# Rotary embedding on one core: loads on SyncE's queue and stores on ScalarE's, in place of both on SyncE's in a fixed order

## The chip, the cores and the metric

The kernel runs on one core of a Trainium2 chip. The metric is the device time of one execution in microseconds. "Before" and "after" are the kernels without and with the change. A core has five engines that run their own programs and meet at semaphores: TensorE (PE), VectorE (DVE), ScalarE (ACT), GpSimd (POOL) and SyncE (SP). Transfers between HBM and the on-chip memory SBUF are issued by an engine's program into that engine's queue, and carried out by 16 DMA engines.

## The reference

The input is 16 batches of 512 positions of 1024 values, which are 16 heads of 64. Each head's first half x1 and second half x2 are rotated by an angle that depends on the position alone; the output has the shape (16, 512, 16, 64), float32.

```python
x = x.reshape(batch, seq, num_heads, head_dim)
x1, x2 = (x[..., :half_dim].copy(), x[..., half_dim:].copy())
cos = cos[None, :, None, :].copy()
sin = sin[None, :, None, :].copy()
rotated = np.concatenate([x1 * cos - x2 * sin, x1 * sin + x2 * cos], axis=-1)
```

## The kernel before

One tile c is one batch: 128 partitions of 4 positions of 1024 values (16 KB per partition, 2 MB in all). A unit u is one of the tile's four rows, 128 x 1024 values; there are NU = 64 units in NC = 16 tiles. The ring x_sb holds 40 units, that is ten tiles; the result is written over the input in the ring and stored from there.

For every unit, t1 = x * cos goes to PSUM (L232, VectorE, "mul") and t2 = swapped x * signed sin goes to t2_sb (L201, GpSimd; for u % 8 = 3, VectorE in L223). Then they are added. For u % 8 in (1, 3, 6) TensorE adds t2 to t1 in PSUM by a matmul with the identity (L172), and ScalarE copies the sum to the ring (L152). For the other units VectorE adds (L243, "comb"). VectorE's program is one list: mul(u), then comb(u - 2), so that the additions of a tile's last two units stand behind the first multiplications of the next tile. A t1 buffer comes free after the addition or the copy of the unit three before it; a t2 buffer after the one six before it.

All transfers are issued by SyncE (on_sync, L120 to L141) into one queue, in an order that is written out: load 0, the two tables, loads 1 to 9, then stores 0, 1 and 2, and from there load c + 8 behind store c for c = 2 to 7, then the stores 8 to 15. A store waits for all additions of its tile (wait_added, L104 to L109: sem_a counts ScalarE's copies, sem_v VectorE's additions). Load c waits from c = 10 on for store c - 10 to land, since it takes that tile's place in the ring. The stores 0 to 5 have semaphores of their own (sem_out), the last ten share sem_rest, for which SyncE waits at its end (L141).

Of the kernel before, what the change touches and what calls it, by code (L numbers as in the profile page):

```python
# [6 lines left out]
def bass_split_heads_rope_kernel(  # L7
# [19 lines left out]
    R = 4  # L27
# [8 lines left out]
    RING = 40  # L36
    NC = batch
    NU = batch * R

    def where(u):  # L40
        return u // R, u % R, u % RING
# [19 lines left out]
    with ExitStack() as stack:  # L61
        x_sb = stack.enter_context(nc.sbuf_tensor([P, RING, H, 2, HALF], fp32))
        t2_sb = stack.enter_context(nc.sbuf_tensor([P, NT2, H, 2, HALF], fp32))
        stage = stack.enter_context(nc.sbuf_tensor([P, 2, R * HALF], fp32))
# [6 lines left out]
        sem_out = [stack.enter_context(nc.semaphore(f"out{c}")) for c in range(NC - RING // R)]  # L71
        sem_rest = stack.enter_context(nc.semaphore("rest"))
        sem_cos = stack.enter_context(nc.semaphore("cos"))
        sem_sin = stack.enter_context(nc.semaphore("sin"))
# [16 lines left out]
        ov = out.rearrange("b (p r) h d -> b p (r h d)", r=R)  # L91
        xs = x_sb[:].rearrange("p n h t d -> p n (h t d)")

        def tile(c):
            k = c * R % RING
            return x_sb[:, k:k + R].rearrange("p n h t d -> p (n h t d)")
# [7 lines left out]
        def wait_added(eng, u):  # L104

            if n_pe[u]:
                eng.wait_ge(sem_a, n_pe[u])
            if n_comb[u]:
                eng.wait_ge(sem_v, n_comb[u])  # L109
# [8 lines left out]
                    eng.wait_ge(sem_v, n_comb[v])  # L118

        def on_sync(sp):  # L120
            AHEAD = 3

            def load(c):
                if c * R >= RING:
                    sp.wait_ge(sem_out[c - RING // R], 16)
                sp.dma_start(tile(c), xv[c]).then_inc(sem_in[c], 16)  # L126

            def store(c):
                wait_added(sp, c * R + R - 1)
                sp.dma_start(ov[c], tile(c)).then_inc(sem_out[c] if c < len(sem_out) else sem_rest, 16)  # L130

            load(0)
            for i, (table, sem) in enumerate(((cos, sem_cos), (sin, sem_sin))):
                sp.dma_start(stage[:, i, :], table.rearrange("(p r) d -> p (r d)", r=R)).then_inc(sem, 16)  # L134
            for c in range(1, RING // R):
                load(c)
            for c in range(NC):
                store(c)
                if AHEAD <= c + 1 < AHEAD + len(sem_out):
                    load(c + 1 - AHEAD + RING // R)  # L140
            sp.wait_ge(sem_rest, 16 * (NC - len(sem_out)))  # L141

        def on_scalar(ae):
            ae.wait_ge(sem_sin, 16)
            sv = stage[:, 1, :].rearrange("s (r d) -> s r d", d=HALF)
            ae.activation(s_sb[:, :, 0, :], sv, COPY, scale=-1.0)  # L146
            ae.activation(s_sb[:, :, 1, :], sv, COPY).then_inc(sem_s, 1)  # L147
            for u in range(NU):
                k = where(u)[2]
                if PE2[u]:  # L150
                    ae.wait_ge(sem_e, n_pe[u])
                    ae.activation(xs[:, k, :], t1_ps[:, u % NT1, :], COPY).then_inc(sem_a, 1)  # L152

        def on_tensor(pe):
            pe.wait_ge(sem_z, 1)
            for k in range(NT1):
                for b in range(EH):
                    pe.matmul(  # L158
                        t1_ps[:, k, b * BANK:(b + 1) * BANK], zero[:, 0:P], zero[:], start=True, stop=True
                    ).then_inc(sem_w, 1)  # L160
            pe.wait_ge(sem_i, 2)
            for u in range(NU):
                if not PE2[u]:
                    continue
                pe.wait_ge(sem_m, u + 1)
                if V2[u]:
                    pe.wait_ge(sem_d, n_dve[u])
                else:
                    pe.wait_ge(sem_p, n_pool[u])
                t2 = t2_sb[:, u % NT2, :, :, :].rearrange("p h t d -> p (h t d)")  # L170
                for b in range(EH):
                    ins = pe.matmul(  # L172
                        t1_ps[:, u % NT1, b * BANK:(b + 1) * BANK],
                        ident[:],
                        t2[:, b * BANK:(b + 1) * BANK],
                        start=False,
                        stop=True,
                        skip_group_check=True,
                    )
                ins.then_inc(sem_e, 1)  # L180
# [24 lines left out]
        def on_vector(ve):  # L205
# [44 lines left out]
            for u in range(NU + LEAD):  # L250
                if u < NU:
                    mul(u)
                if u >= LEAD and not PE2[u - LEAD]:
                    comb(u - LEAD)

        on_sync(nc.sync)
        on_scalar(nc.scalar)
        on_gpsimd(nc.gpsimd)
        on_tensor(nc.tensor)
# [34 lines left out]
```

## Time and profile before

| what | value |
|---|---|
| time, median of 3 runs | 163.88 us (163.47 to 164.49) |
| time of the profiled execution | 163.88 us |
| its span, first to last instruction | 162.5 us |
| DVE busy | 131.9 us (81%) |
| POOL busy | 130.6 us (80%) |
| PE busy | 84.9 us (52%) |
| ACT busy | 26.3 us (16%) |
| bytes moved | 67.26 MB, mean 414 GB/s |
| SyncE's queue, share of the 16 DMA engines' time | 97.7% |
| TensorE's granted clock, mean | 0.657 of full speed |

The span is what the profile covers; the time has a little more around it (163.88 less 162.5 is 1.4 us). A busy time is the union of an engine's own instructions, without its waits. Issuing a transfer isn't counted as busy. "Time to landing" of a transfer runs from its issue until its semaphore is full, and so holds the time that it stood in the queue.

### The profile page before, as it was taken

The page shows a single profiled execution, that of the slowest core. Times are in us where ns is not written, and L with a number is a line of the kernel's source. Part 1 is how long each engine was busy: PE and PEld are TensorE (multiplying, and loading weights), DVE is VectorE, ACT ScalarE, POOL GpSimd, SP SyncE. Part 2 cuts the span into 40 slices and gives each one's busy share as a digit, 9 for nine tenths or more (in the row PEclk, how much of TensorE's full clock was granted, in tenths as well). Part 3 has the DMA queues.
Part 4 walks back from the last instruction along what each step waited for, and adds up shares of the span by engine and source line. Part 5 has one row for each costly group of instructions (what it writes and reads, how often), then busy time and mean ns, then how long its engine had stood idle before and what let it go on. Part 6 is the DMA issues. An engine that isn't in the chain of part 4 may idle for free.

```text
span 162.5 us, 607 instructions
## 1 busy us (share of the span) xinstructions
PE 84.9 (52%) x102; PEld 26.7 (16%) x102; DVE 131.9 (81%) x116; ACT 26.3 (16%) x27; POOL 130.6 (80%) x62
## 2 busy tenths in 40 slices
PE   6003919346746745854745854664864584584000
PEld 1002402211211220220221220121121022021000
DVE  0079299998999979996999789996999899998600
ACT  3010220222022022022202112202102202201200
POOL 1059999999999999999989999799879997970000
PEclk9999995585557655557655558555559555869855
DMA  4999999999999999999999999999999999999993
GB/s 145 403 453 432 420 440 432 415 444 428 411 452 395 436 452 413 424 436 415 430 436 420 420 440 411 424 448 407 432 436 428 424 440 432 415 444 440 411 440 141
DMA packets 4898, 67.26 MB, mean 414 GB/s; under 512 B 544, under 2 KB 800, under 8 KB 800
## 3 DMA queue, kind: packets, MB, share of 16 engines
q1 hardware_dynamic: 4896, 67.24, 97.7%
q14 instruction: 2, 0.02, 0.0%
HBM read 33.69 MB, written 33.55 MB: 414 GB/s over the span
## 4 chain that ended last, share of the span: by engine, by line
DVE 27%; PE 22%; issue 19%; POOL 14%; ACT 6%; DMA 5%; SPq 0%; DVEq 0%; POOLq 0%
PE t_ps L172 22%; DVE x_sb L243 14%; POOL t_sb L201 14%; DVE t_ps L232 9%; ACT x_sb L152 6%; DMA stage<-in_sin_dram 5%; DVE t_sb L223 4%; SPq L134 0%; SPq L126 0%; ACT s_sb L146 0%; ACT s_sb L147 0%; DVEq L242 0%; DVEq L231 0%; DVEq L229 0%; POOLq L116 0%
## 5 line engine op out<-in xcount | busy, mean ns | idle before, releaser
L201 POOL TENSOR_TENSOR t_sb<-x_sb,s_sb 128x1024 f32<-128x1024 f32 x56 | 129.9, 2355 | 13.8 <-ACT s_sb L147 8.6
L172 PE MATMUL t_ps<-t_sb,ident 128*128 128x512 f32 x96 | 82.1, 1009 | 64.1 <-DVE t_ps L232 50.7
L232 DVE TENSOR_TENSOR t_ps<-x_sb,tab_ps 128x1024 f32<-128x1024 f32 x64 | 77.5, 1227 | 12.1 <-ACT x_sb L152 10.1
L243 DVE TENSOR_TENSOR x_sb<-t_ps,t_sb 128x1024 f32<-128x1024 f32 x40 | 48.6, 1217 | 0.0
L172 PEld LDWEIGHTS t_ps<-t_sb,ident 128*128 128x128 f32 x96 | 25.9, 296 | 120.4 <-DVE t_ps L232 85.7
L152 ACT ACTIVATE x_sb<-t_ps 128x1024 f32<-128x1024 f32 x24 | 24.6, 1023 | 116.9 <-PE t_ps L172 116.9
L223 DVE TENSOR_TENSOR t_sb<-x_sb,tab_ps 128x1024 f32<-128x1024 f32 x8 | 9.7, 1210 | 0.0
L210 DVE COPY tab_ps<-stage 128x128 f32<-128x128 f32 x1 | 0.3, 294 | 7.9 <-DMA stage<-in_cos_dram 7.9
L158 PE MATMUL t_ps<-zero 128*128 128x512 bf16 x6 | 2.7, 630 | 1.3 <-DVE zero L206 1.3
L146 ACT ACTIVATE s_sb<-stage 128x128 f32<-128x128 f32 x1 | 0.3, 309 | 7.3 <-DMA stage<-in_sin_dram 7.3
L146 ACT ACT_TABLE_LOAD x1 | 1.3, 1283 | 0.8 <-PEq L276 0.8
L158 PEld LDWEIGHTS t_ps<-zero 128*128 128x128 bf16 x6 | 0.7, 138 | 2.4 <-DVE zero L206 1.2
L206 DVE MEMSET zero<- 128x256 uint32 x1 | 0.3, 272 | 0.9 <-PEq L276 0.9
L183 POOL MEMSET ident<- 128x128 f32 x1 | 0.2, 204 | 0.3 <-POOLq L276 0.3
L185 POOL TENSOR_SCALAR_AFFINE_SELECT ident<-ident 128x128 f32<-128x128 f32 x1 | 0.3, 292 | 0.1
L276 POOL MEMSET const-float32-0.0<- 128x1 f32 x1 | 0.1, 98 | 0.3 <-issue 0.3
L212 DVE TENSOR_SCALAR tab_ps<-stage 128x128 f32<-128x128 f32 x1 | 0.3, 295 | 0.0
L147 ACT ACTIVATE s_sb<-stage 128x128 f32<-128x128 f32 x1 | 0.3, 293 | 0.0
L213 DVE COPY tab_ps<-stage 128x128 f32<-128x128 f32 x1 | 0.3, 283 | 0.0
L276 POOL MEMSET const-bfloat16-1.0<- 128x1 bf16 x1 | 0.1, 101 | 0.0
L276 POOL MEMSET const-uint8-127<- 128x1 uint8 x1 | 0.1, 101 | 0.0
L276 POOL MEMSET const-float32-1.0<- 128x1 f32 x1 | 0.1, 98 | 0.0
## 6 DMA issues: line engine op xcount, KB each, us to landing
x_sb<-in_x_dram SPq DMA_DIRECT2D x16, 2048.0 KB, 25.2
out_dram<-x_sb SPq DMA_DIRECT2D x16, 2048.0 KB, 26.9
stage<-in_cos_dram SPq DMA_DIRECT2D x1, 64.0 KB, 7.9
stage<-in_sin_dram SPq DMA_DIRECT2D x1, 64.0 KB, 7.6
```

The costliest lines, as they stand in the source:

```text
L146: ae.activation(s_sb[:, :, 0, :], sv, COPY, scale=-1.0)
L147: ae.activation(s_sb[:, :, 1, :], sv, COPY).then_inc(sem_s, 1)
L152: ae.activation(xs[:, k, :], t1_ps[:, u % NT1, :], COPY).then_inc(sem_a, 1)
L158: pe.matmul(t1_ps[:, k, b * BANK:(b + 1) * BANK], zero[:, 0:P], zero[:], start=True, stop=True).then_inc(sem_w, 1)
L172: ins = pe.matmul(t1_ps[:, u % NT1, b * BANK:(b + 1) * BANK], ident[:], t2[:, b * BANK:(b + 1) * BANK], start=False, stop=True, skip_group ...
L185: pl.affine_select(out=ident[:], in_=ident[:], compare_op=mybir.AluOpType.is_equal, fill=0.0, base=0, pattern=[[-1, P]], channel_multiplier=1,
L201: pl.tensor_tensor(t2_sb[:, u % NT2, :, :, :], swapped(k), sin_of(s_sb, r), mult).then_inc(sem_p, 1)
L206: ve.memset(zero[:], 0.0).then_inc(sem_z, 1)
L223: ve.tensor_tensor(t2_sb[:, u % NT2, :, :, :], swapped(k), sin_of(s_ps, r), mult).then_inc(sem_d, 1)
L232: ve.tensor_tensor(t1_ps[:, u % NT1, :].rearrange("p (h d) -> p h d", d=HALF), x_sb[:, k, :, :, :].rearrange("p h t d -> p (h t) d"), c_ps ...
L243: ve.tensor_tensor(xs[:, k, :], t1_ps[:, u % NT1, :], t2_sb[:, u % NT2, :, :, :].rearrange("p h t d -> p (h t d)"), add,).then_inc(sem_v, 1)
L276: nc = _bacc.Bacc("TRN2", target_bir_lowering=False, num_devices=1)
```

## The change

SyncE's program now holds the loads alone, in the order of the tiles, with the two tables behind load 0 as before; load c still waits for store c - 10 from c = 10 on. The stores are issued by ScalarE into its own queue: after the last unit of a tile ScalarE waits for all additions of that tile and issues the store. The wait for the last ten stores stays at the end of SyncE's program. No arithmetic is changed: the instructions of TensorE, VectorE and GpSimd are the same and stand in the same order.

```diff
         def on_sync(sp):
-            AHEAD = 3
-
-            def load(c):
+            for c in range(NC):
                 if c * R >= RING:
                     sp.wait_ge(sem_out[c - RING // R], 16)
                 sp.dma_start(tile(c), xv[c]).then_inc(sem_in[c], 16)
-
-            def store(c):
-                wait_added(sp, c * R + R - 1)
-                sp.dma_start(ov[c], tile(c)).then_inc(sem_out[c] if c < len(sem_out) else sem_rest, 16)
-
-            load(0)
-            for i, (table, sem) in enumerate(((cos, sem_cos), (sin, sem_sin))):
-                sp.dma_start(stage[:, i, :], table.rearrange("(p r) d -> p (r d)", r=R)).then_inc(sem, 16)
-            for c in range(1, RING // R):
-                load(c)
-            for c in range(NC):
-                store(c)
-                if AHEAD <= c + 1 < AHEAD + len(sem_out):
-                    load(c + 1 - AHEAD + RING // R)
+                if c == 0:
+                    for i, (table, sem) in enumerate(((cos, sem_cos), (sin, sem_sin))):
+                        sp.dma_start(
+                            stage[:, i, :], table.rearrange("(p r) d -> p (r d)", r=R)
+                        ).then_inc(sem, 16)
             sp.wait_ge(sem_rest, 16 * (NC - len(sem_out)))
 
         def on_scalar(ae):
...
             for u in range(NU):
-                k = where(u)[2]
+                c, r, k = where(u)
                 if PE2[u]:
                     ae.wait_ge(sem_e, n_pe[u])
                     ae.activation(xs[:, k, :], t1_ps[:, u % NT1, :], COPY).then_inc(sem_a, 1)
+                if r == R - 1:
+                    wait_added(ae, u)
+                    ae.dma_start(ov[c], tile(c)).then_inc(sem_out[c] if c < len(sem_out) else sem_rest, 16)
```

## The prediction, made before the changed kernel was run

> **What bounds the kernel now.** I read the page's DMA part first, because a kernel that moves 67 MB and does three elementwise operations per value is likely to stand there.
>
> ```profile
> span 162.5 us, 607 instructions
> ...
> DMA  4999999999999999999999999999999999999993
> ...
> DMA packets 4898, 67.26 MB, mean 414 GB/s; under 512 B 544, under 2 KB 800, under 8 KB 800
> ...
> q1 hardware_dynamic: 4896, 67.24, 97.7%
> ```
>
> All 38 inner slices have the 16 DMA engines at 90% or more, and one queue, SyncE's, carries it all for 97.7% of the span. The kernel is bound by bytes. But what else ends late? The waits of SyncE's queue and two instruction groups tell it.
>
> ```profile
> SPq L109 <- DVE x_sb L243: 73.7, 10, 13.4
> SPq L126 <- DMA out_dram<-x_sb: 52.7, 6, 17.4
> SPq L141 <- DMA out_dram<-x_sb: 9.2, 1, 9.2
> ```
>
> ```profile
> L201 POOL TENSOR_TENSOR t_sb<-x_sb,s_sb 128x1024 f32<-128x1024 f32 x56 | 129.9, 2355 | 13.8 <-ACT s_sb L147 8.6
> ...
> L232 DVE TENSOR_TENSOR t_ps<-x_sb,tab_ps 128x1024 f32<-128x1024 f32 x64 | 77.5, 1227 | 12.1 <-ACT x_sb L152 10.1
> L243 DVE TENSOR_TENSOR x_sb<-t_ps,t_sb 128x1024 f32<-128x1024 f32 x40 | 48.6, 1217 | 0.0
> ```
>
> The reader is to see that the last wait (L141) is 9.2 us, no more than a queued store or two: when the last store is issued, the arithmetic is done and the bytes aren't. POOL is busy 129.9 us and idle 13.8, of which 8.6 come before the tables are there, so arithmetic runs without a pause too. The timeline of SyncE's queue gives its pace: store 0 is issued at 22.2 us, store 13 at 137.92, so (137.92 - 22.2)/13 = 8.9 us per tile, and the last store at 152.92. So two chains end close together: arithmetic at 152.9 and one more store, the bytes at 162.4. A change that helps the bytes soon meets the arithmetic; one that delays the loads soon delays both.
>
> The pace of the bytes comes from issue times and the time to landing, asked for single transfers. Their last lines, for load 1, load 9, store 2, load 15 and store 15, with the issue at 2.18, 6.53, 40.48, 98.49 and 152.92:
>
> ```profile
> DMA to landing us min/median/max: 12.0/12.0/12.0
> DMA to landing us min/median/max: 46.8/46.8/46.8
> DMA to landing us min/median/max: 27.7/27.7/27.7
> DMA to landing us min/median/max: 25.1/25.1/25.1
> DMA to landing us min/median/max: 9.5/9.5/9.5
> ```
>
> They land at 14.2, 53.3, 68.2, 123.6 and 162.4. Eight loads in a row take (53.3 - 14.2)/8 = 4.89 us each. The last eight stores take (162.4 - 123.6)/8 = 4.85. Between them, where load and store take turns, eleven transfers take (123.6 - 68.2)/11 = 5.04, some 0.15 more each. This view of the end shows where that goes:
>
> ```profile
> core 0: us, PE busy (x) PEld busy (x) DVE busy (x) ACT busy (x) POOL busy (x), PEclk, DMA share, GB/s
> ...
> 124.00:152.00 28.00, 15.52 (x20) 4.82 (x20) 26.04 (x24) 5.13 (x6) 19.95 (x9) 0.70 1.00 430
> ...
> 158.00:162.50 4.50, 0.00 (x0) 0.00 (x0) 0.00 (x0) 0.00 (x0) 0.00 (x0) 0.50 0.40 171
> ```
>
> At the end only 0.40 of the engines' time is used: most DMA engines finish near 160, a few near 162.4. These few fell behind in the stretch of turns.
>
> **The change part by part.** *Stores leave SyncE for ScalarE's queue.* Sixteen issues of 0.34 us (median of L130) move. ScalarE is busy 26.3 us, so 16 x 0.34 = 5.4 us fit. What stands behind them is the copy of L152, for which VectorE already waits 10.1 us. Of the three TensorE units in eight, only the one with u % 8 = 1 comes right behind an odd tile's store. That store waits for the addition which VectorE makes directly after the multiplication that starts TensorE: 1.22 us plus 0.34 is 1.6, against up to 3.8 us of matmuls for one unit in the timeline. So the cost is 0, covered by TensorE; were the cover gone, 8 odd tiles x 0.34 = 2.7 us of VectorE. From below, nothing can be gained here. I take 0.
>
> *The wait of the tail.* It stood at the end of SyncE's program (L141) and still stands there; nothing is queued behind it. Cost 0.
>
> *Loads leave the hand-written order.* Load c now waits only for store c - 10, and nothing of SyncE's waits for arithmetic. Before, loads 1 to 9 ran alone until 53.3 us while store 0, issued at 22.2, waited 36.0 us to land. Afterwards store 0 begins near 24. No trace here shows two queues at work together; I bound the sharing by loads first and stores first, and take halves, since loads and stores have packets of one size (67.1 MB in the 4096 that aren't small, 16 KB each). Then load 3 still lands at 24 and load 4 at about 31; after that a load lands every 2 x 4.89 = 9.8 us, load 15 at 31 + 11 x 9.8 = 139 instead of 123.6.
>
> Is that in time? A store hangs on the next load: VectorE's program puts a tile's last additions (L243) behind the first multiplications (L232) of the next tile, so for an odd tile two of each, 4.9 us, and for an even tile 2.4 us, follow the next load. Load 14 (129) allows store 13 at 134, against 137.92 from the pace; load 15 (139) allows store 14 at 142, against 146.96; tile 15 itself needs four of POOL's 2.36 us and an addition, 10.9 us, so 150 against 152.92. Each has 3 to 5 us in hand. Load 10 waits for store 0, which lands near 36, some 45 us before load 10's turn. So nothing starves at halves, and the sum stays with the bytes.
>
> *Turns become a mixture.* From 24 us to load 15, loads 4 to 15 run beside as many stores: 24 transfers instead of 11 in which both directions meet. The nearest row is the stretch of turns, 0.15 us a transfer. Lower bound 0: both directions cost nothing together, and the 11 x 0.15 = 1.7 us of today vanish. Upper bound: the worst step in that stretch, load 13 after store 5 or so, about 5.4 us against 4.89, is 0.5 each, 12 us. I take 0.15, because it is a mean over eleven: 24 x 0.15 = 3.6, less today's 1.7, makes +1.9 us. With it load 15 lands near 142.5, and tile 15 would be stored at 153.4 where the pace says 152.9: the two meet, and starving adds at most 0.5, which the queue's own backlog covers.
>
> The sum: 162.5 + 1.9 = 164.4 us of span. The profiled execution took 163.88, so 1.4 us lie around the span; it is also the median of the runs (163.47 to 164.49). Forecast 165.8 us.
>
> A rule speaks against the 0.15. The Trainium skill, page "DMA: Bandwidth & Descriptors", section "Latency and other measured facts", has copies of this very tile size through sync and scalar queues at 214 GB/s in each direction at once, when the rows don't alias. That would be 428 GB/s in sum, the rate that the windows above show for stores alone (430), and hence no price for the mixture; the sum by the rule would be 162.1. The same page, section "Queues, rings and completion order", lets each DMA engine take its queues in turn, packet by packet, which would make my halves right; no trace here shows it yet.
>
> **The rivals.**
>
> *Stores crowd out loads (slower still).* If the second queue gets more than half, stores take all that arithmetic hands them: 4.9 of every 8.9 us, and a load lands every 8.9/4.0 x 4.9 = 10.9 us. Load c + 1 then overtakes the pace: it lands at 33 + 10.9 (c - 3), and 4.9 us later must not exceed 22.2 + 8.9c, which fails from c = 9. From there every tile costs two transfers, 9.8 us: store 14 at 102.3 + 5 x 9.8 = 151, tile 15 at 160, its store lands 7 later, 167; with the mixture's 1.9, 169, in time 170.4. For it: POOL has hardly any idle time to catch up with. Against it: equal packets, and a starving arithmetic hands out fewer stores, which gives the loads room.
>
> *The mixture is free, or better than turns (faster).* The place is the end, the 4.5 us with 0.40 of the DMA engines. If each DMA engine always has work of both kinds, none need fall behind, and today's 1.7 us go: 160.7 of span, 162.1 in time. It can't get much lower: arithmetic ends at 152.9 and one store alone takes 4.9 us plus issue and completion (load 0, the only transfer into an idle queue, took 8.1 in all), some 160. The case decides when the mixture costs under 0.02 us a transfer (24 x 0.02 = 0.5 against 1.7, that is 161.3). For it: at 124 to 152 the engines run at 1.00 without any loss, while a few still lag 3 us. Against it: only unmixed stretches are without loss.
>
> *Nothing changes.* The same bytes at the same share, between 0.02 and 0.13 us a transfer: span 161.3 to 163.9, times 162.7 to 165.3. For it: 97.7% of DMA time is used either way.
>
> *ScalarE as the new bottleneck.* If an issue blocks as load 9's did (2.08 us, with nine transfers ahead of it), 8 x (1.22 + 2.08 - 3.8), which is below 0, still hides; only with faster matmuls (2 us) does it cost 8 x 1.3 = 10 us. The store queue never holds more than two or three, so I give it little: some 171.
>
> **How the numbers follow.** A measurement of this kernel can tell about 1% from no change, 1.6 us. Forecast (mixture at 0.13 to 0.3 us a transfer, 165.3 to 169.4): 0.42. Stores crowding out loads: 0.10. ScalarE: 0.03. Mixture free: 0.15. Nothing changes: 0.30. Within 1% means 162.2 to 165.5, so 0.02 of the forecast and 0.01 of the free mixture count to the middle: faster 0.14, same 0.33, slower 0.53. The likeliest one's own range is 165.3 to 169.4; the whole one goes from 161.8 (between the free mixture's 162.1 and its floor, 160 and 1.4) to 170.5 (stores first).
>
> **What would show it.** Right: two queues with about half the packets each, load 15 landing at 139 to 143, loads that land before arithmetic asks for them, the last store issued at 152 to 154, transfers in the mixed stretch costing 5.0 us each, and some DMA engines more than 3 us behind at the end. Wrong: POOL idle for loads in the second half (stores first), VectorE's wait for ScalarE well over 10.1 us, an end near 160.5 with an even finish of the DMA engines, or a pace of packets in the mixture that isn't that of either stretch before.

## The result, and the profile after

The changed kernel takes 161.97 us (161.75 to 162.11, 4 runs) against 163.69 (163.47 to 164.49, 4 runs) for the kernel before: a ratio of 0.9885, 95% interval 0.9848 to 0.9922. It is 1.2% faster, where 1.2% slower was forecast. The profiled executions took 161.94 and 163.88 us, with spans of 160.5 and 162.5: 2.0 us less.

The page of the kernel after, the lines that answer to those of before:

```profile
span 160.5 us, 607 instructions
...
DMA  5999999999999999999999999999999999999996
...
DMA packets 4899, 67.27 MB, mean 419 GB/s; under 512 B 544, under 2 KB 800, under 8 KB 800
...
q1 hardware_dynamic: 2592, 33.69, 49.9%
q10 hardware_dynamic: 2304, 33.56, 48.8%
...
L193 POOL TENSOR_TENSOR t_sb<-x_sb,s_sb 128x1024 f32<-128x1024 f32 x56 | 129.6, 2376 | 17.0 <-DMA x_sb<-in_x_dram 8.9
L224 DVE TENSOR_TENSOR t_ps<-x_sb,tab_ps 128x1024 f32<-128x1024 f32 x64 | 77.1, 1227 | 10.4 <-ACT x_sb L141 8.6
```

Two queues now carry half of the bytes each, with the DMA engines at 90% or more in every inner slice, as before. POOL waits 8.9 us for loads, for which it never waited before; VectorE waits 8.6 us for ScalarE, no more than the 10.1 of before.

The pace in the mixture, from loads 4 and 15 (issued at 3.87 and 86.17 us), and the end, from store 15 (issued at 150.47). The last line of each answer has the time from issue to landing:

```profile
DMA to landing us min/median/max: 27.3/27.3/27.3
DMA to landing us min/median/max: 52.5/52.5/52.5
DMA to landing us min/median/max: 10.0/10.0/10.0
```

Load 4 lands at 31.2, load 15 at 138.7, store 15 at 160.5. Eleven loads and as many stores share (138.7 - 31.2) = 107.5 us, 4.89 per transfer. That is the pace of loads alone before (4.89) and not that of the turns (5.04). The busy time by stage shows where the two kernels differ. First before, the stretch of turns and two windows at the end of the span:

```profile
core 0: us, PE busy (x) PEld busy (x) DVE busy (x) ACT busy (x) POOL busy (x), PEclk, DMA share, GB/s
...
68.00:124.00 56.00, 33.33 (x38) 9.86 (x36) 51.14 (x45) 10.22 (x10) 51.87 (x23) 0.57 1.01 427
...
160.00:161.00 1.00, 0.00 (x0) 0.00 (x0) 0.00 (x0) 0.00 (x0) 0.00 (x0) 0.50 0.31 131
161.00:162.50 1.50, 0.00 (x0) 0.00 (x0) 0.00 (x0) 0.00 (x0) 0.00 (x0) 0.50 0.05 22
```

and after, the mixture and the end:

```profile
core 0: us, PE busy (x) PEld busy (x) DVE busy (x) ACT busy (x) POOL busy (x), PEclk, DMA share, GB/s
...
40.00:124.00 84.00, 49.11 (x59) 15.38 (x60) 79.33 (x69) 14.32 (x14) 78.33 (x35) 0.63 1.01 431
158.00:160.50 2.50, 0.00 (x0) 0.00 (x0) 0.00 (x0) 0.00 (x0) 0.00 (x0) 0.50 0.51 216
...
160.00:161.00 1.00, 0.00 (x0) 0.00 (x0) 0.00 (x0) 0.00 (x0) 0.00 (x0) 0.50 0.00 0
```

From 160 to 161 us the DMA share before is still 0.31, the work of five of the 16 engines, when the others have finished; after, it is 0.00. The rates in the middle hardly differ, 427 GB/s in the turns and 431 in the mixture: only a few engines fall behind, and the end waits for them. The trace has each DMA engine's own landing as well: of the last store, the first engine lands at 159.48 us in both kernels, the last one at 162.44 before and at 160.50 after. So 1.94 of the 2.0 us are DMA engines that no longer fall behind.

### The profile page after: what moved, and what is told of

It reads as the page before. It is cut to its first block, busy times and chain, and to the rows that moved or that the text cites. A ratio compares the mean times of both kernels' runs of the same rounds, so it can differ in the third digit from the quotient of the medians.

```text
span 160.5 us, 607 instructions
## 1 busy us (share of the span) xinstructions
PE 81.7 (51%) x102; PEld 25.4 (16%) x102; DVE 131.5 (82%) x116; ACT 26.3 (16%) x27; POOL 130.3 (81%) x62
## 4 chain that ended last, share of the span: by engine, by line
DVE 36%; PE 19%; issue 17%; POOL 10%; ACT 5%; DMA 5%; SPq 0%; DVEq 0%; POOLq 0%
PE t_ps L164 19%; DVE x_sb L235 18%; DVE t_ps L224 15%; POOL t_sb L193 10%; ACT x_sb L141 5%; DMA stage<-in_sin_dram 5%; DVE t_sb L215 4%; SPq L127 0%; SPq L124 0%; ACT s_sb L135 0%; ACT s_sb L136 0%; DVEq L234 0%; DVEq L223 0%; POOLq L116 0%; DVEq L221 0%
## 5 line engine op out<-in xcount | busy, mean ns | idle before, releaser
L164 PE MATMUL t_ps<-t_sb,ident 128*128 128x512 f32 x96 | 78.9, 972 | 65.8 <-DVE t_ps L224 49.8
L164 PEld LDWEIGHTS t_ps<-t_sb,ident 128*128 128x128 f32 x96 | 24.7, 281 | 119.4 <-DVE t_ps L224 86.4
```

Of the source, the lines that this page charges most:

```text
L164: ins = pe.matmul(t1_ps[:, u % NT1, b * BANK:(b + 1) * BANK], ident[:], t2[:, b * BANK:(b + 1) * BANK], start=False, stop=True, skip_group ...
```

## The experiments

Three theories stood at the start. A: each change of direction within a queue costs something. B: the second queue as such helps. C: stores gain by beginning 31 us earlier. A turn is what a queue moves in one direction before it changes to the other. The first table is the theories' measure: when the first and the last DMA engine land their part of the last transfer, in the profiled execution; the lag is the difference. The ratios below are to the kernel before in the same round of runs.

| kernel | queues, order | first engine | last engine | lag |
|---|---|---|---|---|
| before | one, 13 changes of direction | 159.48 | 162.44 | 2.96 |
| after | two, by direction | 159.48 | 160.50 | 1.02 |
| one_blocks | one, 3 changes | 159.62 | 160.84 | 1.22 |
| one_turns | one, 23 changes | 159.47 | 162.84 | 3.37 |
| two_late2 | two, stores begin at 45 us | 159.56 | 160.67 | 1.11 |
| copy_one | transfers of before alone | 159.34 | 162.63 | 3.29 |
| copy_two | transfers of after alone | 159.79 | 160.37 | 0.58 |
| copy_turns | transfers of one_turns alone | 159.62 | 162.75 | 3.13 |
| copy_rows2 | 8 KB packets, turns of 2 MB | 161.50 | 164.33 | 2.83 |
| copy_rows1 | 8 KB packets, turns of 1 MB | 160.88 | 161.57 | 0.69 |

The packets in the traces of before and after show what the lag is made of. A packet of 16 KB takes 0.61 us. After the first 20 us, 41 packets of before take over 0.66 us, 11.0 us too long together, and none of them begins after 124 us, where the turns end. A packet's engine can be inferred, since it begins as the last one on its engine ends. By that, 40 of the 41 belong to loads 9 to 15, which have a store next behind them in the queue, and none to loads 3 to 8, which have not; the five engines that end last hold 9.3 of the 11.0 us. After has 32 such packets, 29 of them between 24 and 28 us, where the first store meets the loads, and no engine has more than 0.84 us of them. From 50 to 135 us the two queues of after take turns of one packet: in all 1793 cases in which a packet's follower on its engine is certain, it is of the other queue. So a DMA engine falls behind by single slow load packets, mostly ahead of a store. Why these are slow was not found.

**Blocks in one queue (one_blocks).** Against the kernel before:

```diff
-            for c in range(NC):
-                store(c)
-                if AHEAD <= c + 1 < AHEAD + len(sem_out):
-                    load(c + 1 - AHEAD + RING // R)
+            for c in range(len(sem_out)):
+                store(c)
+            for c in range(RING // R, NC):
+                load(c)
+            for c in range(len(sem_out), NC):
+                store(c)
```

> One queue still, all on SyncE, but loads and stores in blocks: loads 0 to 9, stores 0 to 5, loads 10 to 15, stores 6 to 15. The direction changes 3 times in place of 13. Theory A (each change of direction in the queue costs, because some DMA engines fall behind there; 1.7 us over the 13): span 162.5 - 1.7 x 10/13 = 161.2, time about 162.6, last store issued at 151 to 153. Theory B (a second queue is what helps: with one queue every transfer of the middle stretch costs 0.15 more): unchanged, span 162.5, time 163.7. Theory C (the gain came from stores starting 31 us earlier): unchanged or later, since load 10 waits for the stores.

Measured: 162.15 us, ratio 0.9908 (0.9889 to 0.9927), near A's 162.6 and against B and C. The page shows one queue and nearly the whole gain:

```profile
span 160.9 us, 607 instructions
...
q1 hardware_dynamic: 4896, 67.24, 98.5%
```

The last store was issued at 153.50, a little later than expected, and landed 7.3 us later: here arithmetic and bytes end together. A second queue is not needed for the gain.

**Turns all the way in one queue (one_turns).** Loads 0 to 4, then:

```diff
-            for c in range(1, RING // R):
+            for c in range(1, FIRST):
                 load(c)
             for c in range(NC):
                 store(c)
-                if AHEAD <= c + 1 < AHEAD + len(sem_out):
-                    load(c + 1 - AHEAD + RING // R)
+                if c + FIRST < NC:
+                    load(c + FIRST)
```

> One queue, all on SyncE, turns all the way: loads 0 to 4, then store c and load c + 5 in turn to the end of the loads, then stores 11 to 15. The direction changes 23 times in place of 13, and the loads land at the pace that they had in the changed kernel. Theory A (changes of direction cost): 10 x 1.7/13 = 1.3 us more than before, span 163.8, time 165.2. Theory B (second queue): span 162.5, time 163.7. Theory C (early stores): as the changed kernel, span 160.5, time 162.0.

Measured: 164.47 us, ratio 1.0056 (1.0034 to 1.0078). The sign is A's, and C falls: its loads land at the changed kernel's pace and its stores begin nearly as early, yet it is slower than before. The size is not A's: 162.9 of span instead of 163.8. By the trace the lag grows to 3.32 us until store 7 lands, and then stays between 3.32 and 3.38 through the eight further changes. So the cost of a change is not a constant, and A needed mending.

**Late stores in two queues (two_late, two_late2).** First ScalarE was made to wait for load 9 ahead of store 0:

```diff
                 if r == R - 1:
+                    if c == 0:
+                        ae.wait_ge(sem_in[RING // R - 1], 16)
                     wait_added(ae, u)
```

> The changed kernel, but ScalarE holds store 0 back until load 9 has landed (53 us), so that stores start as late as they do before the change. Theories A and B (mixture of two queues costs nothing): span 160.5, time 162.0. Theory C (early start of the stores): span near 162.5, time 163.7. If holding the stores delays later loads so far that arithmetic starves, VectorE's or POOL's waits for loads show it.

Measured: 185.38 us, ratio 1.1258. The experiment failed as a test of C, because the wait held back what stands behind it on ScalarE. Four of its longest waits:

```profile
...
ACT x_sb L141 <- PE t_ps L166: 102.8, 22, 8.7
...
ACT x_sb L141 <- DMA x_sb<-in_x_dram: 32.4, 1, 32.4
...
DVE t_ps L226 <- ACT x_sb L141: 31.7, 8, 25.6
POOL t_sb L195 <- DVE x_sb L237: 26.2, 7, 22.0
```

ScalarE stood 32.4 us for the load, VectorE then up to 25.6 us for ScalarE's copy, POOL up to 22.0 for VectorE: the same delay handed on three times. The second form delays the stores by their place in ScalarE's program alone:

```diff
-                if r == R - 1:
-                    wait_added(ae, u)
-                    ae.dma_start(ov[c], tile(c)).then_inc(...)
+                if r == R - 1 and c >= 3:
+                    for d in range(4) if c == 3 else (c,):
+                        wait_added(ae, d * R + R - 1)
+                        ae.dma_start(ov[d], tile(d)).then_inc(...)
```

> The changed kernel, but ScalarE issues the stores 0 to 3 together at the place of store 3 in its program (about 48 us), without a wait of their own, so that its copies go on and the stores start some 26 us later. Mixture free, whenever it begins: span 160.5, time 162.0. The early start is the cause: most of the gain is lost, span near 162.

Measured: 162.22 us, ratio 0.9917 (0.9895 to 0.994), span 160.7. The first store is issued at 45.0 us in place of 22.1, and most of the gain is there. C has failed in three runs: one_blocks, one_turns and this one.

**The transfers alone (copy_one, copy_two, copy_turns).** The arithmetic is left out and each store waits for its load only; queues and orders are those of before, after and one_turns.

```diff
             def store(c):
-                wait_added(sp, c * R + R - 1)
+                sp.wait_ge(sem_in[c], 16)
```

> The transfers of the kernel before alone: the same loads, tables and stores on SyncE's queue in the same order, with the arithmetic left out (what is stored is the input) and stores waiting for their load only. If the loss at the changes of direction lies in the transfers themselves, span about 162 as before, the middle stretch at 5.0 us a transfer and the last landings of one transfer spread over some 3 us. If it comes from the engines' traffic to SBUF beside the transfers, the stretch goes at 4.87 and the span is near 160.5.

> The transfers of the changed kernel alone: loads on SyncE's queue, stores on ScalarE's, arithmetic left out (what is stored is the input), each store waiting for its load only. Theory A and B: 4.87 us a transfer throughout, span near 160.3, about 2 us under the transfers in one queue. If the engines' traffic made the difference: no difference between the two.

Measured: copy_one 163.71 us (ratio 0.9986, 0.9969 to 1.0002), copy_two 161.82 (0.9874, 0.9858 to 0.9891), spans 162.7 and 160.4. Without any arithmetic the two orders differ by 1.9 us, as the whole kernels do by 1.7, and each time is within 0.2 us of the whole kernel's. The loss lies in the transfers, and both kernels are bound by them to within 0.2 us of span.

**How long a turn is (copy_turns, copy_half, copy_rows2, copy_rows1).** Theory A2 took A's place: a DMA engine falls behind only until it is out of step with the others by some part of a turn, so that the lag is bounded by the turn's length.

> One queue on SyncE, transfers alone (arithmetic left out, what is stored is the input): loads 0 to 4, then store c and load c + 5 in turn. It stands as the base for the next two. Span near 162.8 as with arithmetic, first and last landing of the last store 3.3 us apart.

> As copy_turns (arithmetic left out), but each transfer is split into two of 64 partitions and the turns are of 1 MB: twice as many changes of direction, packets of 16 KB still. Theory A (each change costs some): at least as late as copy_turns, span 163 or more. Theory A2 (the DMA engines that fall behind stop doing so once they are out of step with the others by a part of a turn, so the lag is bounded by the length of a turn): lag about half, 1.7 us, span near 161.3.

Measured: copy_turns 164.24 us, span 162.8, lag 3.13: the base holds. copy_half took 244.81 us (a second execution 236.56), a span of 243.4, and told nothing of A2, for another reason: a load of 64 partitions took as long as one of 128 (the second load of tile 1 lands 4.96 us behind the first, for 1 MB). So the halves were cut by rows in place of partitions:

```diff
-                sp.dma_start(tile(c), xv[c]).then_inc(sem_in[c], 16)
+                w = slice(h * HW, (h + 1) * HW)
+                sp.dma_start(tile(c)[:, w], xv[c][:, w]).then_inc(sem_in[c], 16)
```

> Transfers alone (arithmetic left out, what is stored is the input), one queue, each transfer split into two of 128 partitions and two of the four rows, packets of 8 KB; both halves of store c, then both of load c + 5: turns of 2 MB as in copy_turns. Base for the next one. Lag of the last store's landings 3.3 us as in copy_turns if the packet's size plays no part.

> The same halves (arithmetic left out), but a half of store c and a half of load c + 5 in turn: turns of 1 MB, 45 changes of direction in place of 23. Theory A (each change costs some): the lag grows past copy_rows2's, the span is 1 us or more later. Theory A2 (the lag is bounded by the length of a turn, since engines that are out of step no longer fall behind): lag about half of copy_rows2's, 1.7 us, span some 1.5 us earlier.

Measured: copy_rows2 165.84 us (ratio 1.011, 1.0078 to 1.0142), copy_rows1 162.89 (0.9928, 0.9906 to 0.9951). With the same transfers in the same queue, twice as many changes of direction are 2.95 us faster (165.84 - 162.89); the spans are 164.4 and 161.6, the lags 2.83 and 0.69. A is refuted, and A2's direction is shown: shorter turns leave less lag. Its size is not: half the lag was expected, and with 1 MB turns the lag does not grow at all (load 1, ahead of any store, has 0.87 us, the last store 0.69). After 20 us, the trace of copy_rows1 has slow packets (over 0.36 us where an 8 KB packet takes 0.31) only between 25 and 28 us, ahead of the first change, and none through the 44 changes behind it. The lag accounts for 2.14 of the 2.8 us of span; the first engine also ends 0.62 earlier.

**Two queues that are not split by direction (copy_parity).** Even tiles' loads and stores on SyncE's queue, odd ones' on ScalarE's, transfers alone.

> Transfers alone (arithmetic left out) in two queues, but not split by direction: SyncE issues loads and stores of even tiles in turn, ScalarE those of odd tiles. If two queues at work together are enough: span near 160.4 as with loads and stores apart. If each queue must hold one direction: the changes of direction within each queue cost as with one, span near 162.5.

Its profiled execution has a span of 160.5 us and a time of 161.84; a second one took 164.56. One execution is a hint that two queues suffice whatever their directions, and no more. It was not followed up.

## Why the prediction was wrong

*The step that failed* is the last of the sum, "Turns become a mixture": "24 x 0.15 = 3.6, less today's 1.7, makes +1.9 us". The mixture costs nothing over loads alone: 4.89 us a transfer, so the term is 0 and today's loss goes, 1.94 us by the lag: the term is -1.9 us in place of +1.9. The prediction had seen that a few engines fall behind, and yet priced every transfer with it. In the stretch of turns (store 2 to load 15) the first engine to land took 4.82 us a transfer and the last one 5.03, so the 0.15 was no price of each transfer but a lag that grew from 0.68 to 2.98 us. The error was to carry a mean per transfer from turns of 2 MB to turns of one packet. It rested on "the nearest row", but that row was near in direction and far in length; copy_rows1 against copy_rows2 shows that the cost per change falls when turns go from 2 MB to 1 MB, by more than the number of changes rises. The lower bound of the same term, 0, was right.

*The rival* "The mixture is free" had the place (the engines that finish late), the mechanism (none need fall behind) and the numbers: 160.7 of span and 162.1 us against 160.5 and 161.97. It had 0.15 of the chances, and was counted against with "only unmixed stretches are without loss", which the trace of before could not tell, since it held no other mixture. The page of the Trainium skill that was weighed there, "DMA: Bandwidth & Descriptors", section "Latency and other measured facts", spoke for it, and the trace agrees: 431 GB/s in the mixture, against the 214 per direction that the page has for such copies, 428 in sum.

*What was right.* One bound by bytes, the other close behind it: the first DMA engine ends at 159.48 in both. Halves as the sharing: load 4 was put at "about 31" and landed at 31.2, load 15 at 139 (without the mixture's cost) and landed at 138.7, store 0 was put at 36 and landed at 37.5. ScalarE's issues cost VectorE nothing: it waits 8.6 us for ScalarE, where it waited 10.1. No cost of the tail's wait shows.

*What was right by luck or short.* The "about 31" for load 4 does not follow from halves that begin at 24 us, which give 24 + 9.8 = 33.8; the first packet of a store came at 25.8, and halves from there do give 31. Load 15's 139 was counted from the 31, so its place is in part luck, while the pace, 9.8 us a load, was right (9.77). Two slips change nothing: four of POOL's 2.36 us and an addition are 10.7, not 10.9, and the step of about 5.4 us was load 14's, while load 13's took 5.1. That "nothing starves" is not quite so: POOL waits for loads five times, 8.9 us in all, and its idle time is now 17.0 instead of 13.8. It did not reach the end: the last store was issued at 150.47, earlier than the 152.92 of before. Why arithmetic ended earlier was not tested. TensorE's granted clock in the two executions was 0.702 and 0.657; one_turns, at 0.698, issued its last store at 150.68, two_late2, at 0.664, at 153.38, and one_blocks, at 0.646, at 153.50. The two early ones have the higher clocks, but also the latest loads (load 15 at 138.6 in both), so these traces do not tell the two apart.

*No version beats the changed kernel clearly.* The transfers alone, copy_two, need 160.4 us of span, against its 160.5. What is left is the start before the first packet (1.8 us), the packets themselves, and an uneven finish of about 1 us.

## What to carry to other kernels

In a kernel bound by transfers, compare the first and the last DMA engine's landing of the last transfer: of that difference a better order won back 1.94 of 2.96 us here, while the total of bytes set the rest. Loads and stores that alternate in one queue in large turns cost such a lag; few large blocks, or two queues at work together, avoided most of it here, each for about 1% of the time, and so did turns of 1 MB with the transfers alone. A cost per change of direction must not be carried to turns of another length, and a wait that is meant for a store alone must not stand in front of an engine's copies.

## What the runs showed of the hardware

- Loads and stores from two queues at once shared the DMA engines in halves, packet by packet, at 4.89 us per 2 MB transfer, the pace of loads alone.
- In one queue with turns of 2 MB some DMA engines fell behind by up to 3.4 us, and in one_turns no further through the last eight changes; with turns of 1 MB (copy_rows1) the lag did not grow. It needs no arithmetic beside it.
- They fell behind by single slow packets, in before 41 of over 0.66 us in place of 0.61, all but one in loads with a store next behind them. What makes these slow was not found.
- A packet of 8 KB took 0.309 us (median, copy_rows1 and copy_rows2) against 0.611 for 16 KB, 1.1% more per byte; the first DMA engine finished at 161.50 in place of 159.62 (copy_rows2 against copy_turns), 1.2% later.
- A load of 1 MB into 64 partitions took 4.96 us (copy_half), about as long as 2 MB into 128 (4.89).
